# Hybrid encoder block on one core: who issues the stores of the FFN products, and when the residual is fetched

## Chip, cores and metric

The kernel runs on one core of a Trainium2 chip. The metric is the device time of one execution in microseconds. A core has a matrix engine (TensorE, here PE), three engines for element-wise work (VectorE or DVE, ScalarE or ACT, GpSimd or POOL) and SyncE (SP), which in this kernel only issues DMAs. Each engine works through its own instructions in order, and so does the queue of DMAs that an engine issues; an instruction whose wait isn't over holds all that stands behind it on its engine.

## What is computed

One encoder block on x of 1024 x 1024 floats: a SwiGLU FFN half, two token mixers with a merge, a second FFN half, a gated projection of per-layer embeddings p, and a final norm. D_FF is 2816.

```python
h = x
h = h + 0.5 * swiglu(rms_norm(h, ffn1_norm), ffn1_w_gate, ffn1_w_up, ffn1_w_down)
u = rms_norm(h, mix_norm)
...                                   # attention, retention, merge: h = h + merged @ w_out
h = h + 0.5 * swiglu(rms_norm(h, ffn2_norm), ffn2_w_gate, ffn2_w_up, ffn2_w_down)
gate = sigmoid(rms_norm(h, ple_norm) @ w_ple_gate)
h = h + gate * (p @ w_ple_proj)
return rms_norm(h, final_norm)

def swiglu(x, w_gate, w_up, w_down):
    return (silu(x @ w_gate) * (x @ w_up)) @ w_down
```

## The kernel before

**Matrix products.** Every float product is made of three matmuls: each operand is split into a high part h and a rest l, and h·h, h·l and l·h are added. Weights go through the class `Weights`. A load brings a piece of 128x1024 from memory into one of a few raw buffers (`wraw`); a fill splits it into a slot's `wh` (ACT, L144) and `wl` (DVE, L146; for some jobs POOL). Loads run as far ahead as raw buffers are free, fills as far as slots are free. `matrix` (L168 on) takes two raw pieces, top and bottom, and has POOL make two more from them, sums (L184, L185) and differences (L192, L193): seven factors in four fills.

**The FFN halves.** `Seven` computes each FFN as block products of two by two with seven products instead of eight. Its stage `products` runs over 11 pairs `j` of 256 of the 2816 columns: 14 products of 12 matmuls each (168), first for the gate, then for up. ACT moves the first part of a sum out of PSUM (`ev`, L576), DVE adds the others (L580), ACT applies silu (L602), DVE multiplies by up (L605). That gives four gated blocks `g` of 128x512. POOL makes three combinations of them (L627 to L630), and SP stores seven factors in memory, `hf` (L633). For the pair's part of the down matrix, `down_factors` loads four tiles `wd` (L645, SP), POOL makes four differences (L646 to L649), and SP stores them, `wf` (L651). The stage `down` then runs seven products (A11, A12, S2, S1, S3, S4, A22), each over the 11 `j` with 12 matmuls (132); it loads the stored factors again through `Weights.plain` (L155). The results are added to the residual `hres` (L672), which is x itself in FFN1 and a stored h in FFN2. The stages of FFN1 lie from about 68 to 532 us (products) and from there (down) in the profile, those of FFN2 from 1853 and from 2321 us.

**Head.** Ahead of the first products stage x is normed and turned, and p is projected: 16 blocks, which ACT takes from PSUM and SP stores in `ppspill` (L759, L760).

**Order.** PE runs in program order. On the other engines a scheduler sets the order from the program; on each DMA queue the issues stand in that order. So a load on SP stands behind whatever store was put ahead of it, and a store waits on SP until its data are made. Residual loads stand in the program ahead of `down`: 16 of 128x512 (L796 in FFN1, L1548 in FFN2).

Of the kernel before, what the change touches and what calls it, by code (L numbers as in the profile page):

```python
# [277 lines left out]
def hybrid_block_kernel(  # L278
# [29 lines left out]

    LEFT = ["A11", "A12", "S2", "S1", "S3", "S4", "A22"]
# [3 lines left out]
    def seven_jobs(name, wg, wu, wd):  # L313
# [9 lines left out]
        for a in LEFT:  # L323
            for j in range(NJ2):
                q = LEFT.index(a)
                t = {"S1": 0, "S2": 1, "S3": 2, "A22": 3}.get(a)
                if t is None:
                    f, c = {"A11": (0, 0), "A12": (1, 0), "S4": (1, 512)}[a]
                    wap = krows(wd, c, c + 512, 2 * j + f, 2 * j + f + 1)
                else:  # L330
                    wap = wsp[name][j][:, t:t + 1]
                W.plain((name, a, j), 1, D, False, [(0, 512, hsp[name][j][:, q:q + 1]), (512, D, wap)])
# [150 lines left out]
    class Seven:  # L483
# [66 lines left out]
        def products(self, between):  # L550
# [8 lines left out]
            g = {0: [ev.tile([P, 512], F32, name=f"g{i}") for i in range(4)]}  # L559
# [47 lines left out]
            for j in range(NJ2):  # L607
                h = g[j % 2]
# [9 lines left out]
                if j == 0:  # L618
                    self.top.close()
                    sp = self.top.enter_context(tc.tile_pool(name="hid2", bufs=1, side="right"))  # L620
                    g[1] = [sp.tile([P, 512], F32, name=f"g{i}") for i in range(4)]
                for _ in up or blocks("u", j, times(h)):
                    pass
                s1, s2, s4 = (sp.tile([P, 512], F32, name=f"s{i}", tag="s", bufs=8) for i in range(3))
# [6 lines left out]
                made = dict(A11=h11, A12=h21, S2=s2, S1=s1, S3=h12, S4=s4, A22=h22)  # L631
                for q, n in enumerate(LEFT):
                    nc.sync.dma_start(hsp[self.name][j][:, q], made[n])  # L633
                self.down_factors(sp, j)
# [4 lines left out]
        def down_factors(self, pool, j):  # L639

            gp = nc.gpsimd
            b11, b12, b21, b22 = t = [pool.tile([P, 512], F32, name=f"wd{i}", tag="s", bufs=8) for i in range(4)]
            for i in range(4):
                c0 = 512 * (i % 2)
                nc.sync.dma_start(t[i], krows(self.wd, c0, c0 + 512, 2 * j + i // 2, 2 * j + i // 2 + 1)[:, 0])  # L645
            gp.tensor_tensor(b11, b12, b11, op=OP.subtract)  # L646
            gp.tensor_tensor(b12, b22, b12, op=OP.subtract)  # L647
            gp.tensor_tensor(b22, b22, b11, op=OP.subtract)  # L648
            gp.tensor_tensor(b21, b21, b22, op=OP.subtract)  # L649
            for q, d in enumerate((b11, b22, b12, b21)):  # L650
                nc.sync.dma_start(wsp[self.name][j][:, q], d)  # L651

        def down(self, hres, finished, turn, other={}):
# [3 lines left out]
            def run(a, ps, start, stop, between=None):  # L657
                for j in range(NJ2):
                    key = self.name, a, j
                    h, l = (x[:, 0] for x in W[key])  # L660
                    for i in range(4):
# [12 lines left out]
            run("A11", sums, True, False)  # L674
            to(sums, 0, 0)
            pc = [bank("dn", "pdc") for _ in range(4)]
            run("A12", pc, True, True)
            to(pc, 0, 0)
            run("S2", sums, False, False)
            to(sums, 0, 1)  # L680
            pc = [bank("dn", "pdc") for _ in range(4)]
            run("S1", pc, True, False)
# [39 lines left out]
    order = [b + 4 * e for b in range(4) for e in range(2)]  # L722
    W.limit = 2
    W.load()
    load_p(0)
    seven.open()
    for b in order[:2]:
        load_x(b)
    seven.load_gain()
    W.load()  # L730
    load_p(2)
    for b in order[2:4]:
        load_x(b)
    nc.vector.memset(mhalf, -0.5)
# [19 lines left out]
    def proj_p(b, i):  # L754
# [5 lines left out]
        nc.sync.dma_start(ppspill[:, b, half(i)], t)  # L760
# [33 lines left out]
    for i in range(2):  # L794
        for b in range(NB):
            nc.sync.dma_start(hres[:, b, half(i)], x0[tok(b), half(i)])  # L796
# [59 lines left out]
    seven.down(hres, finished, turn, {4: lambda: W.drop(raws)})  # L856
# [689 lines left out]
    for i in range(2):  # L1546
        for b in range(NB):
            nc.sync.dma_start(hres[:, b, half(i)], h2spill[:, b, half(i)])  # L1548
# [13 lines left out]
    seven.down(hres, finished, turn)  # L1562
# [85 lines left out]
```

## Time and profile before

| | us |
|---|---|
| median of 3 runs (2648.21 to 2649.6) | 2648.36 |
| the profiled execution | 2651.99 |
| its span | 2650.2 |

| engine | busy us | share of span |
|---|---|---|
| PE | 2489.3 | 94% |
| DVE | 1514.1 | 57% |
| ACT | 1100.8 | 42% |
| POOL | 899.4 | 34% |

The mean granted clock of PE is 0.975 of full speed, 2.4 GHz. A busy share is a mean over stages with different limits: PE at 94% says that the engine is rarely idle, and the waits of PE say where it is. All DMAs of this kernel are issued by hardware queues (272,064 packets, 347.27 MB); POOL issues none. Times in the trace are from the start of the span.

### The profile page before, as it was taken

What the parts mean: (1) busy time and instruction counts of PE and PEld (TensorE: products, weight loads), DVE (VectorE), ACT (ScalarE), POOL (GpSimd) and SP (SyncE); (2) the same over time, 40 slices, a digit from 0 to 9 for tenths busy, and PEclk for the clock granted to TensorE, in tenths of its full rate; (3) what the DMA queues carried; (4) which work ended last, traced back from release to release, by engine and by line L of the source; (5) the groups of instructions that cost most, each with busy time, mean ns of one, the idle gap of its engine ahead of it and who ended that gap; (6) DMA issues with size and microseconds to landing.
All of it is one profiled execution on the core that took longest, in us unless ns stands there. A gap on an engine that the chain in (4) does not pass through costs nothing. (4 is left out here: it accounts for less than half of the span.)

```text
span 2650.2 us, 32857 instructions
## 1 busy us (share of the span) xinstructions
PE 2489.3 (94%) x11464; PEld 2030.7 (77%) x11464; DVE 1514.1 (57%) x2640; ACT 1100.8 (42%) x1900; POOL 899.4 (34%) x688
## 2 busy tenths in 40 slices
PE   6999999989999998989999999998999999989998
PEld 5777777768888777767878887787777777768887
DVE  5444444455567879997457664635444444445564
ACT  5333333334355667652235653414323233334452
POOL 5356565410000333343443431004456565410000
PEclk8999999989999999989999999999999999989999
DMA  5244344576640221221221218642244444586632
GB/s 194 92 135 158 130 146 139 172 261 212 192 155 21 84 81 33 68 80 44 86 82 37 82 61 244 183 161 82 94 133 147 130 156 138 174 296 203 196 98 95
DMA packets 272230, 349.36 MB, mean 132 GB/s; under 512 B 22976, under 2 KB 152256, under 8 KB 272064
## 3 DMA queue, kind: packets, MB, share of 16 engines
q1 hardware_dynamic: 272064, 347.27, 41.3%
q8 instruction: 90, 1.47, 0.2%
q14 instruction: 76, 0.62, 0.1%
HBM read 246.00 MB, written 101.19 MB: 131 GB/s over the span
## 5 line engine op out<-in xcount | busy, mean ns | idle before, releaser
L146 DVE TENSOR_TENSOR wl<-wraw,wh 128x1024 fp32r<-128x1024 f32 (+2 forms) x422 | 521.0, 1241 | 542.9 <-ACT wh L144 528.2
L144 ACT ACTIVATE wh<-wraw 128x1024 fp32r<-128x1024 f32 (+1 forms) x466 | 436.5, 938 | 852.1 <-PE pc L565 195.1
L439 PE MATMUL prod<-wh,uh 128*128 128x512 f32 (+1 forms) x648 | 266.6, 411 | 0.2 <-ACT gt L1036 0.2
L439 PE MATMUL prod<-wh,ul 128*128 128x512 f32 (+1 forms) x648 | 257.8, 398 | 0.0
L439 PE MATMUL prod<-wl,uh 128*128 128x512 f32 (+1 forms) x648 | 257.3, 397 | 0.0
L565 PE MATMUL pa<-th,wh 128*128 128x512 f32 x352 | 142.8, 406 | 43.2 <-ACT ev L576 43.2
L1029 PE MATMUL pgate<-uh,wh 128*128 128x512 f32 x384 | 159.2, 415 | 20.9 <-ACT gt L1036 19.8
L663 PE MATMUL pda<-wh 128*128 128x512 f32 x352 | 140.3, 399 | 21.4 <-ACT wh L144 10.7
L465 POOL TENSOR_TENSOR nst<-nst,mhalf 128x1 f32<-128x1 f32 x16 | 8.7, 550 | 443.6 <-DVE nst L464 443.6
L1029 PE MATMUL pgate<-uh,wl 128*128 128x512 f32 x384 | 154.5, 402 | 0.0
L1029 PE MATMUL pgate<-ul,wh 128*128 128x512 f32 x384 | 154.4, 402 | 0.0
L439 PEld LDWEIGHTS prod<-wh,ul 128*128 128x128 f32 x648 | 123.7, 191 | 29.2
L565 PE MATMUL pa<-ul,wh 128*128 128x512 f32 x352 | 141.2, 401 | 4.7 <-DVE ul L402 4.7
L1096 ACT ACTIVATE bias<-bias 128x1024 bf16<-128x1024 bf16 (+3 forms) x132 | 117.3, 890 | 63.0 <-DVE bias L1095 61.7
L146 POOL TENSOR_TENSOR wl<-wraw,wh 128x1024 fp32r<-128x1024 f32 x44 | 109.7, 2496 | 98.5 <-ACT wh L144 97.9
L565 PE MATMUL pa<-th,wl 128*128 128x512 f32 x352 | 142.7, 405 | 0.0
L565 PE MATMUL pa<-uh,wh 128*128 128x512 f32 x352 | 140.6, 399 | 1.8 <-ACT uh L401 1.8
L565 PE MATMUL pa<-tl,wh 128*128 128x512 f32 x352 | 142.0, 403 | 0.0
L663 PE MATMUL pda<-wl,wh 128*128 128x512 f32 x352 | 139.5, 396 | 2.5 <-DVE wl L146 2.5
L565 PE MATMUL pa<-uh,wl 128*128 128x512 f32 x352 | 140.8, 400 | 0.0
L565 PE MATMUL pc<-uh,wl 128*128 128x512 f32 x352 | 139.7, 397 | 0.0
L565 PE MATMUL pc<-ul,wh 128*128 128x512 f32 x352 | 139.6, 396 | 0.0
(274 smaller groups left out, 6008.0 us busy)
## 6 DMA issues: line engine op xcount, KB each, us to landing
wraw<-hf SPq DMA_DIRECT2D x154, 256.0 KB, 3.0
wraw<-in_ffn_w_gate_dram SPq DMA_DIRECT2D x44, 512.0 KB, 5.2
wraw<-in_ffn_w_up_dram SPq DMA_DIRECT2D x44, 512.0 KB, 3.8
hf<-g SPq DMA_DIRECT2D x88, 256.0 KB, 2.3
wd<-in_ffn_w_down_dram SPq DMA_DIRECT2D x88, 256.0 KB, 4.3
wf<-wd SPq DMA_DIRECT2D x88, 256.0 KB, 2.6
wraw<-wf SPq DMA_DIRECT2D x88, 256.0 KB, 3.2
hf<-s SPq DMA_DIRECT2D x66, 256.0 KB, 2.0
```

The costliest lines, as they stand in the source:

```text
L144: self.nc.scalar.activation(h, src, AF.Copy)
L146: eng.tensor_tensor(l, src, h.bitcast(F32), op=OP.subtract)
L439: nc.tensor.matmul(box[0][:, :cols], a, w, start=k == 0 and i == 0, stop=k == nk - 1 and i == 2)
L465: nc.gpsimd.tensor_tensor(st[:, 1:2], st[:, 0:1], mhalf, op=OP.pow)
L565: nc.tensor.matmul(ps, x_, y_, start=start and k == 0 and i == 0, stop=stop and k == 3 and i == 2, skip_group_check=True)
L663: nc.tensor.matmul(ps[i], x_, y_, start=start and j == 0 and n == 0, stop=stop and j == NJ2 - 1 and n == 2, skip_group_check=True)
L1029: nc.tensor.matmul(box[0], a, m, start=k == 0 and j == 0, stop=k == KT - 1 and j == 2)
L1096: nc.scalar.activation(m, m, AF.Copy, accum_out=cnt[:, j:j + 1])
```

## The change

It changes who issues the stores, in what pieces, and where some loads stand.

1. In `products` the four `g` blocks become one tile, the three combinations two tiles, and the stored order of the factors (`HID`) is made to fit: POOL stores them with three DMAs per pair (1 MB, 512 KB, 256 KB) where SP had seven of 256 KB.
2. The `wd` loads go into a function of their own, `down_rows`, called ahead of the up blocks; they are four of 256 KB in runs of 1 KB. The differences become eight operations of 128x256, and POOL stores them with two DMAs per pair instead of four on SP.
3. The 16 residual loads become four groups of four, each at `j` = 4 of one of the first four runs of `down`. A copy of one column (128x1) on POOL out of the weights in use, ahead of each load, holds it until then.
4. `ppspill` is stored by ACT instead of SP.
5. At the start the loads of p and x stand in another order.

```diff
+    HID = ["A11", "S3", "A12", "A22", "S2", "S1", "S4"]
...
-                q = LEFT.index(a)
-                t = {"S1": 0, "S2": 1, "S3": 2, "A22": 3}.get(a)
+                q = HID.index(a)
+                t = {"S1": 0, "S3": 1, "A22": 2, "S2": 3}.get(a)
...
-            g = {0: [ev.tile([P, 512], F32, name=f"g{i}") for i in range(4)]}
+            g = {0: ev.tile([P, 4, 512], F32, name="g0")}
...
-                    g[1] = [sp.tile([P, 512], F32, name=f"g{i}") for i in range(4)]
+                    g[1] = sp.tile([P, 4, 512], F32, name="g1")
+                wd = self.down_rows(sp, j)
-                s1, s2, s4 = (sp.tile([P, 512], F32, name=f"s{i}", tag="s", bufs=8) for i in range(3))
+                sa, sb = (sp.tile([P, 2, 512], F32, name=f"s{i}", tag="s", bufs=5) for i in range(2))
+                s2, s1, s4 = sa[:, 0], sa[:, 1], sb[:, 0]
-                made = dict(A11=h11, A12=h21, S2=s2, S1=s1, S3=h12, S4=s4, A22=h22)
-                for q, n in enumerate(LEFT):
-                    nc.sync.dma_start(hsp[self.name][j][:, q], made[n])
-                self.down_factors(sp, j)
+                to = hsp[self.name][j]
+                gp.dma_start(to[:, 0:4], g[j % 2])
+                gp.dma_start(to[:, 4:6], sa)
+                gp.dma_start(to[:, 6], s4)
+                self.down_factors(wd, j)
-        def down_factors(self, pool, j):
+        def down_rows(self, pool, j):
+            wd = [pool.tile([P, 2, 2, 256], F32, name=f"wd{i}", tag="s", bufs=5) for i in range(2)]
+            for q in range(2):
+                for f in range(2):
+                    rows = krows(self.wd, 0, D, 2 * j + f, 2 * j + f + 1)[:, 0].rearrange("p (i c) -> p i c", i=2)
+                    nc.sync.dma_start(wd[q][:, f], rows[:, :, 256 * q:256 * q + 256])
+            return wd
+        def down_factors(self, wd, j):
-            b11, b12, b21, b22 = t = [pool.tile([P, 512], F32, name=f"wd{i}", tag="s", bufs=8) for i in range(4)]
-            for i in range(4):
-                c0 = 512 * (i % 2)
-                nc.sync.dma_start(t[i], krows(self.wd, c0, c0 + 512, 2 * j + i // 2, 2 * j + i // 2 + 1)[:, 0])
-            gp.tensor_tensor(b11, b12, b11, op=OP.subtract)
-            gp.tensor_tensor(b12, b22, b12, op=OP.subtract)
-            gp.tensor_tensor(b22, b22, b11, op=OP.subtract)
-            gp.tensor_tensor(b21, b21, b22, op=OP.subtract)
-            for q, d in enumerate((b11, b22, b12, b21)):
-                nc.sync.dma_start(wsp[self.name][j][:, q], d)
-        def down(self, hres, finished, turn, other={}):
+            for q in range(2):
+                b11, b12, b21, b22 = (wd[q][:, i // 2, i % 2] for i in range(4))
+                gp.tensor_tensor(b11, b12, b11, op=OP.subtract)
+                gp.tensor_tensor(b12, b22, b12, op=OP.subtract)
+                gp.tensor_tensor(b22, b22, b11, op=OP.subtract)
+                gp.tensor_tensor(b21, b21, b22, op=OP.subtract)
+                gp.dma_start(wsp[self.name][j][:, :, 256 * q:256 * q + 256],
+                             wd[q].rearrange("p f i c -> p (f i) c"))
+        def down(self, hres, residual, finished, turn, other={}):
-            def run(a, ps, start, stop, between=None):
+            def fetch(t, i):
+                def go(h):
+                    for b in range(4 * t, 4 * t + 4):
+                        nc.gpsimd.tensor_copy(hres[:, b, 512 * i:512 * i + 1], h[:, 0:1].bitcast(F32))
+                        nc.sync.dma_start(hres[:, b, half(i)], residual(b, i))
+                return go
+            def run(a, ps, start, stop, between=None, load=None):
+                    if load and j == 4:
+                        load(h)
...
-            run("A11", sums, True, False)
+            run("A11", sums, True, False, load=fetch(0, 0))
-            run("A12", pc, True, True)
+            run("A12", pc, True, True, load=fetch(0, 1))
-            run("S2", sums, False, False)
+            run("S2", sums, False, False, load=fetch(1, 1))
-            run("S1", pc, True, False)
+            run("S1", pc, True, False, load=fetch(1, 0))
...
     order = [b + 4 * e for b in range(4) for e in range(2)]
+    seven.open()
+    load_p(0)
+    W.limit = 1
+    W.load()
+    load_x(order[0])
+    load_x(order[1])
+    seven.load_gain()
     W.limit = 2
     W.load()
-    load_p(0)
-    seven.open()
-    for b in order[:2]:
-        load_x(b)
-    seven.load_gain()
-    W.load()
-    load_p(2)
     for b in order[2:4]:
         load_x(b)
+    load_p(2)
     nc.vector.memset(mhalf, -0.5)
...
-        nc.sync.dma_start(ppspill[:, b, half(i)], t)
+        nc.scalar.dma_start(ppspill[:, b, half(i)], t)
...
-    for i in range(2):
-        for b in range(NB):
-            nc.sync.dma_start(hres[:, b, half(i)], x0[tok(b), half(i)])
...
-    seven.down(hres, finished, turn, {4: lambda: W.drop(raws)})
+    seven.down(hres, lambda b, i: x0[tok(b), half(i)], finished, turn, {4: lambda: W.drop(raws)})
...
-    for i in range(2):
-        for b in range(NB):
-            nc.sync.dma_start(hres[:, b, half(i)], h2spill[:, b, half(i)])
```

Three places show how this moves instructions: a pair of the products on SP and on POOL, the start of `down` on SP, and the head on DVE. A row is the line, the operation, what it writes and reads, and the shape of a tile; names carry a number, rows of a kernel its own lines. First SP in a middle pair of FFN1's products: `wd` are the tiles of the down matrix, `wf11` the stored factors of a pair, `wraw` the raw weight buffers. Before:

```order
L645 DMA wd0_1200<-in_ffn1_w_down_dram 128x512
L645 DMA wd1_1201<-in_ffn1_w_down_dram 128x512
L645 DMA wd2_1202<-in_ffn1_w_down_dram 128x512
L645 DMA wd3_1203<-in_ffn1_w_down_dram 128x512
L172 DMA wraw0_135<-in_ffn1_w_gate_dram 128x4x256
L651 DMA wf11_87<-wd0_1200 128x512
L651 DMA wf11_87<-wd1_1201 128x512
L651 DMA wf11_87<-wd3_1203 128x512
L651 DMA wf11_87<-wd2_1202 128x512
L172 DMA wraw1_136<-in_ffn1_w_gate_dram 128x4x256
L172 DMA wraw0_135<-in_ffn1_w_up_dram 128x4x256
```

After:

```order
L648 DMA wd0_1316<-in_ffn1_w_down_dram 128x2x256 x2
L172 DMA wraw0_135<-in_ffn1_w_gate_dram 128x4x256
L648 DMA wd1_1317<-in_ffn1_w_down_dram 128x2x256 x2
L172 DMA wraw1_136<-in_ffn1_w_gate_dram 128x4x256
L172 DMA wraw0_135<-in_ffn1_w_up_dram 128x4x256
L172 DMA wraw0_65<-in_ffn1_w_up_dram 128x4x256
```

The two gate loads had four `wd` loads ahead of the first and four factor stores between them; now there are two `wd` loads ahead of each, and no store.

On POOL in the same place, from the first combination of `g` on; L184, L185, L192 and L193 are the sums and differences of raw weights, `hf11` the stored gated factors, `s` the combinations. Before:

```order
L627 TENSOR_TENSOR s0_1186<-g1_840,g3_842 128x512
L628 TENSOR_TENSOR s1_1187<-s0_1186,g0_839 128x512
L629 TENSOR_TENSOR g1_840<-g0_839,g1_840 128x512
L184 TENSOR_TENSOR wraw1_136<-wraw0_135,wraw1_66 128x512
L185 TENSOR_TENSOR wraw1_136<-wraw1_136,wraw0_135 128x512
L630 TENSOR_TENSOR s2_1188<-g2_841,s1_1187 128x512
L193 TENSOR_TENSOR wraw0_65<-wraw1_66,wraw1_136 128x512
L646 TENSOR_TENSOR wd0_1200<-wd1_1201,wd0_1200 128x512
L647 TENSOR_TENSOR wd1_1201<-wd3_1203,wd1_1201 128x512
L648 TENSOR_TENSOR wd3_1203<-wd3_1203,wd0_1200 128x512
L649 TENSOR_TENSOR wd2_1202<-wd2_1202,wd3_1203 128x512
L192 TENSOR_TENSOR wraw1_66<-wraw0_135 128x512
```

After:

```order
L630 TENSOR_TENSOR s0_1181<-g1_836 128x512
L631 TENSOR_TENSOR s0_1181<-s0_1181,g1_836 128x512
L632 TENSOR_TENSOR g1_836<-g1_836 128x512
L184 TENSOR_TENSOR wraw1_136<-wraw0_135,wraw1_66 128x512
L636 DMA hf11_76<-s0_1181 128x1024
L185 TENSOR_TENSOR wraw1_136<-wraw1_136,wraw0_135 128x512
L633 TENSOR_TENSOR s1_1182<-g1_836,s0_1181 128x512
L193 TENSOR_TENSOR wraw0_65<-wraw1_66,wraw1_136 128x512
L635 DMA hf11_76<-g1_836 128x2048
L637 DMA hf11_76<-s1_1182 128x512
L656 TENSOR_TENSOR wd0_1316<-wd0_1316 128x256
L192 TENSOR_TENSOR wraw1_66<-wraw0_135 128x512
```

Three store issues now stand between POOL's operations, one ahead of the second sum L185 and two ahead of the `wd` work; the `wd` work that begins here is that of the next pair's `wd`, and its two stores follow behind these rows, ahead of the next L184.

SP where `down` of FFN1 begins; `hf` and `in_ffn1_w_down` are the loads of stored factors and of the down matrix, `cs` a table for later. Before:

```order
L651 DMA wf110_96<-wd3_3563 128x512
L651 DMA wf110_96<-wd2_3562 128x512
L155 DMA wraw0_135<-in_ffn1_w_down_dram 128x512
L155 DMA wraw0_65<-hf19_84 128x512
L155 DMA wraw0_65<-in_ffn1_w_down_dram 128x512
L796 DMA hres_3605<-in_x_dram 128x512 x16
L797 DMA cs_3597<-in_cst_dram 128x616
L155 DMA wraw1_66<-in_ffn1_w_down_dram 128x512
L155 DMA wraw1_136<-hf10_75 128x512
```

After:

```order
L815 DMA cs_3536<-in_cst_dram 128x616
L155 DMA wraw0_135<-hf18_83 128x512
L155 DMA wraw0_135<-in_ffn1_w_down_dram 128x512
L155 DMA wraw0_65<-hf19_84 128x512
L155 DMA wraw0_65<-in_ffn1_w_down_dram 128x512
L155 DMA wraw1_136<-in_ffn1_w_down_dram 128x512
L672 DMA hres_3544<-in_x_dram 128x512 x3
L155 DMA wraw0_135<-hf11_76 128x512
L155 DMA wraw0_135<-in_ffn1_w_down_dram 128x512
L155 DMA wraw0_65<-hf12_77 128x512
L155 DMA wraw0_65<-in_ffn1_w_down_dram 128x512
```

The 16 residual loads stood together behind two factor stores and ahead of the weight loads for later `j`; now three of the first four stand behind six or more of those loads, and no store is in the row.

DVE in the head, around the scaling of one x tile (`xt_491`, whose factor `nst_512` POOL makes): L402 before and L403 after is the split of turned blocks for PE. Before:

```order
L402 TENSOR_TENSOR tl_147<-ntr_426,th_146 128x4x128
L402 TENSOR_TENSOR tl_147<-ntr_443,th_146 128x4x128
L516 TENSOR_SCALAR nst_512<-nst_512 128x1
L518 SCALAR_TENSOR_TENSOR xt_491<-xt_491,nst_512,gain_155 128x1024
L402 TENSOR_TENSOR tl_147<-ntr_460,th_146 128x4x128
L402 TENSOR_TENSOR ul_121<-ntr_467,uh_120 128x4x128
L402 TENSOR_TENSOR ul_121<-ntr_484,uh_120 128x4x128
L402 TENSOR_TENSOR pt1_508<-ptr_502,pt0_507 128x512
```

After:

```order
L403 TENSOR_TENSOR tl_144<-ntr_426,th_143 128x4x128
L403 TENSOR_TENSOR tl_144<-ntr_443,th_143 128x4x128
L403 TENSOR_TENSOR tl_144<-ntr_460,th_143 128x4x128
L403 TENSOR_TENSOR ul_121<-ntr_467,uh_120 128x4x128
L403 TENSOR_TENSOR ul_121<-ntr_484,uh_120 128x4x128
L403 TENSOR_TENSOR pt1_508<-ptr_502,pt0_507 128x512
L517 TENSOR_SCALAR nst_512<-nst_512 128x1
L519 SCALAR_TENSOR_TENSOR xt_491<-xt_491,nst_512,gain_155 128x1024
```

The pair of `nst_512` and `xt_491` stood ahead of four splits and now stands behind them.

## Rows read from the trace of the kernel before

**Rows 1.** The page's first part: busy us (share of the span), instructions.

```profile
PE 2489.3 (94%) x11464; PEld 2030.7 (77%) x11464; DVE 1514.1 (57%) x2640; ACT 1100.8 (42%) x1900; POOL 899.4 (34%) x688
```

**Rows 2.** PE's waits, two windows: us in total, times, longest.

```profile
PE pa L565 <- ACT ev L576: 20.9, 9, 2.7
...
PE pa L565 <- ACT ev L576: 22.3, 9, 4.2
```

**Rows 3.** Stretches: length, engines' busy us (instructions), PEclk, DMA share, GB/s.

```profile
142.60:479.60 337.00, 318.20 (x1344) 255.26 (x1344) 152.98 (x161) 105.83 (x161) 193.62 (x129) 0.98 0.44 144
...
479.60:532.50 52.90, 52.89 (x229) 42.96 (x230) 24.87 (x29) 16.58 (x24) 20.09 (x15) 1.00 0.52 171
...
532.50:579.90 47.40, 34.47 (x133) 26.18 (x132) 18.42 (x26) 12.55 (x12) 12.75 (x8) 0.87 0.83 279
...
1930.40:2268.70 338.30, 319.29 (x1344) 256.07 (x1344) 151.29 (x161) 105.85 (x161) 193.84 (x129) 0.98 0.44 143
...
2321.60:2365.60 44.00, 32.96 (x133) 26.39 (x132) 13.06 (x13) 11.27 (x12) 10.89 (x8) 0.84 0.91 313
...
2365.60:2395.50 29.90, 29.90 (x133) 24.75 (x133) 20.65 (x20) 14.78 (x14) 0.00 (x0) 1.00 0.79 262
```

**Rows 4.** PE's timeline, one pair: start, us, instruction [idle before <-releaser].

```profile
310.31 0.50 PE L565 MATMUL pa<-th,wh 128*128 128x512 f32 x1 [2.74 <-ACT ev L576]
```

**Rows 5.** ACT's timeline, the same pair.

```profile
308.13 0.63 ACT L144 ACTIVATE wh<-wraw 128x512 fp32r<-128x512 f32 x1 [7.50 <-DMA wraw<-in_ffn_w_gate_dram]
```

**Rows 6.** Timeline of SP's queue, the same pair.

```profile
291.59 1.87 SPq L645 DMA_DIRECT2D wd<-in_ffn_w_down_dram  x4
...
293.56 0.38 SPq L172 DMA_DIRECT2D wraw<-in_ffn_w_gate_dram  x1
...
297.61 6.04 SPq L651 DMA_DIRECT2D wf<-wd  x4
...
303.74 0.39 SPq L172 DMA_DIRECT2D wraw<-in_ffn_w_gate_dram  x1
```

**Rows 7.** DVE's timeline, the same pair.

```profile
294.59 1.23 DVE L146 TENSOR_TENSOR wl<-wraw,wh 128x1024 fp32r<-128x1024 f32 x1 [4.55 <-ACT wh L144]
```

**Rows 8.** POOL: timeline of that pair; groups (busy, mean ns | idle, releaser).

```profile
281.25 2.21 POOL L627 TENSOR_TENSOR s<-g,g 128x512 f32<-128x512 f32 x1 [5.94 <-DVE g L605]
...
309.53 1.62 POOL L185 TENSOR_TENSOR wraw<-wraw,wraw 128x512 f32<-128x512 f32 x1
...
L629 POOL TENSOR_TENSOR g<-g,g 128x512 f32<-128x512 f32 x11 | 14.2, 1295 | 0.0
...
L146 POOL TENSOR_TENSOR wl<-wraw,wh 128x1024 fp32r<-128x1024 f32 x44 | 109.7, 2496 | 98.5 <-ACT wh L144 97.9
```

**Rows 9.** Timelines from products to down: PE, SP, ACT, POOL.

```profile
573.71 0.80 PE L663 MATMUL pda<-wh 128*128 128x512 f32 x1 [9.37 <-ACT wh L144]
...
555.49 10.41 SPq L796 DMA_DIRECT2D hres<-in_x_dram  x16
...
572.60 1.06 ACT L144 ACTIVATE wh<-wraw 128x1024 fp32r<-128x1024 f32 x1 [13.74 <-DMA wraw<-in_ffn_w_down_dram]
...
532.48 2.20 POOL L627 TENSOR_TENSOR s<-g,g 128x512 f32<-128x512 f32 x1 [19.89 <-DVE g L605]
...
2320.47 2.22 POOL L627 TENSOR_TENSOR s<-g,g 128x512 f32<-128x512 f32 x1 [17.61 <-DVE g L605]
```

**Rows 10.** DMA issues: KB each, median us from issue to landing.

```profile
hspill<-hres SPq DMA_DIRECT2D x8, 512.0 KB, 5.3
...
hf<-g SPq DMA_DIRECT2D x88, 256.0 KB, 2.3
```

**Rows 11.** Timelines of the head: PE, DVE.

```profile
53.01 1.12 PE L749 MATMUL ptr<-ident,praw 128*128 128x128 f32 x4 [5.73 <-DVE tl L402]
...
51.07 1.28 DVE L518 SCALAR_TENSOR_TENSOR xt<-xt,nst,gain 128x1024 f32<-128x1024 f32 x1 [3.91 <-POOL nst L517]
...
52.27 0.69 DVE L402 TENSOR_TENSOR tl<-ntr,th 128x512 fp32r<-128x512 f32 x1
```

More of the change, by code (lines that the diff above doesn't have):

```diff
@@ L607, in products @@
             for j in range(NJ2):
-                h = g[j % 2]
+                h = [g[j % 2][:, i] for i in range(4)]
                 gate, up = blocks("g", j, silu(h)), None
@@ L1561, in hybrid_block_kernel @@
     finished = normed(ple_norm[0], hres)
-    seven.down(hres, finished, turn)
+    seven.down(hres, lambda b, i: h2spill[:, b, half(i)], finished, turn)
     ph = ExitStack()
```

## Prediction

> **What bounds the kernel now.** I read the page's first part, PE's waits, tables by stage, and then one wait along its chain. The page's first part says that TensorE (PE) is busy 94% of the span [rows 1]: nothing shortens this kernel but filling PE's gaps, so an engine or a queue matters only where PE waits for it. The table of PE's waits, taken over each of the two products stages, shows one kind: PE at L565 waits for ScalarE's (ACT) eviction `ev`, nine times in each stage, 43.2 us together [rows 2], once per pair `j`. The tables by stretch price this. Eight pairs are 8 x 168 = 1344 matmuls and take 337.00 us in FFN1, 338.30 in FFN2; the stretch behind the first, without such a wait, 479.60 to 532.50, runs its 228 whole matmuls (229 shown, one cut by the edge) in 52.90 us, 0.232 each [rows 3]. At that rate 1344 take 311.8. So 25.2 and 26.5 us are lost, 51.7 over 16 pairs, **3.2 us for each**: about 2.3 of wait (43.2/18), the other 0.9 of work after it at a lower granted clock (0.98 against 1.00 over the stretch). Two further stretches are slow: the first run (A11) of each "down" stage, 132 matmuls, takes 47.40 and 44.00 us, at clock 0.87 and 0.84, where the run after it takes 29.90 at 1.00 [rows 3]. That is 17.5 and 14.1 lost.
>
> **Why PE waits in a pair.** Follow the one at 310.31 [rows 4]. ACT works in order. It is free from 300.6, but the next on it is the fill `wh<-wraw`, which waits 7.50 us for the pair's second gate load and starts at 308.13; the `ev` that PE needs stands behind that fill [rows 5]. SP issued that load at 303.74, though it issued the first at 293.56. Between them stand four stores of down factors, which hold SP from 297.61 to 303.65 [rows 6], because they wait for POOL's differences of `wd`, themselves waiting for loads issued only at 291.59. The raw buffer that the load fills was free at about 295.8, when DVE's `wl<-wraw` of 294.59 ended [rows 7].
>
> **Products, after.** The factor stores go to POOL and the `wd` loads go ahead of the up blocks, so SP has nothing between the two gate loads that waits for POOL's arithmetic; it keeps only two `wd` loads, whose buffers were stored from a pair earlier (some 40 us). The load goes out at about 296, when its buffer is free, and lands after its 4.4 us (303.74 to 308.13) at 300.4: as ACT comes to it at 300.6. ACT then gains 7.5 us and PE needs 2.3: the wait is gone, and the clock's share with it. ACT keeps 5 us of cover for what is late next, POOL (below). I take 3.0 of the 3.2, for 18 pairs: **54 us**.
>
> POOL is the price. It is busy 193.62 us in the eight pairs, 24.2 per pair [rows 3]. The eight half-wide `wd` operations I take as the four whole ones. Added are five DMA issues per pair. No row shows what POOL pays for one, X: the low end is what SP pays, 0.39 for a load [rows 6]; the high end is POOL's longest operation, 2.50 (L146, 128x1024); I take one POOL pass over a 512-wide tile, 1.30 (L629) [rows 8], since 128 to 512 descriptors are more than SP's one instruction and less than a pass over 1024. Then POOL has 24.2 + 6.5 = 30.7 per pair, under PE's 39.0 (168 x 0.232), and costs nothing on the average. Nearer is the order: all five issues stand ahead of the sums L184/L185 that feed a later fill of ACT. POOL starts the pair's chain at 281.25; its seven operations took to 292.4 (L627 2.21, the others 1.3 to 1.7), and with three issues (3.9) it is at 296.3; L192 (1.3), the `wd` work (6.0) and two issues (2.6) bring it to 306.2, the two sums to 309.1. Before, L185 ended at 311.15 and no PE wait came from it [rows 8]. So there are 2 us of room at least, and I guess twice that: X up to 1.7 to 2.2 is covered, beyond it ACT waits again. The same shape takes 2.21 us at L627 and 1.30 at L629 [rows 8]: something stretches POOL. Beside that stands the Trainium skill, "SBUF — State Buffer", section "SBUF: two separate sides": a DMA issued by GpSimd has its descriptors written by GpSimd, which some two-port DVE operations lock out; the same page gives 620 ns alone and 3100 ns beside such an operation. By 3.1 for every issue POOL would have 24.2 + 15.5 = 39.7 per pair, just over PE's 39.0; no run here shows it yet.
>
> SP loses eleven issues a pair (19 to 8); it doesn't bind, so that is worth nothing by itself. The larger stores and the 1 KB runs of `wd` move the same bytes; the DMA share is 0.44 in these stretches [rows 3], so nothing.
>
> **Down stages.** In FFN1 SP issues 16 residual loads from 555.49 to 565.90, behind two factor stores that wait for POOL; the first weight load comes after them, ACT's fill waits 13.74 us for it, and PE waits 9.37 at 573.71 [rows 9]. After, four residual loads stand at each of four later points, behind weight loads, and no store is on SP. What is late next: the fill of `j` = 4 goes into memory that held the last `g`, so it waits for the last `g` store, which POOL now issues behind its arithmetic. POOL starts L627 at 532.48 [rows 9]; three operations of 2.2, 2.2 and 1.3, another issue of 1.3 and L630's 1.3 bring the issue to about 541; 1 MB I estimate to land in 4 us, between 2.3 for 256 KB and 5.3 for 512 KB [rows 10]; then ACT's 1.06 and DVE's 1.23 [rows 9, 7]: 547.7. PE needs it at 532.5 + 48 x 0.232 = 543.6: a wait of 4.1, and some 1.5 of lower clock (at 0.9 for 2.3, as above). FFN1 gains 17.5 - 5.6 = 11.9. In FFN2 POOL starts its chain at 2320.47 [rows 9], 1.1 us ahead of the run, so 3.0 and 1.1 stay, and 10.0 are gained. Together **22 us**; bounds 2 (X of 2.5 and the 1 MB at four times 2.3 make either wait 7.6 longer) and 32 (all of it).
>
> **Head.** DVE's scaling at 51.07, which waits for POOL, stands ahead of the split at 52.27 for which PE waits 5.73 [rows 11]; DVE's new order puts four splits before it. Late `x` loads no longer stand behind spill stores on SP. Against that ACT issues the 16 spill stores, at 0.39 some 6 us of ACT work. I take **3**, bounds -4 (they fall on ACT where PE waits) and +6 (the wait).
>
> **Sum:** 54 + 22 + 3 = 79. The profiled execution lasted 2651.99 (span 2650.2): 2573. The median of the runs is 3.6 lower: 2569, so **2570**.
>
> **Rival B, another wait takes its place.** The pair's wait stays: X is 2.2 to 3.5, L185 comes late, ACT now waits for POOL's sums as it did for the load, and PE waits for `ev` as before. Only the other two gains are left: 2648.4 - 25 = **2624**; a half-way case lies near 2600. For it: POOL's longer operations, and cover of only 2 to 4 us. Against it: POOL is idle for 14.8 of a pair's 39.0 now. Here stands a rule of the Trainium skill, "DMA: Bandwidth & Descriptors", section "Issuing engines are not separate DMA queues": issuing from several engines saves only the time that the issue takes, usually small. By it the move to POOL would be worth little and 2624 the time. The trace speaks against it: the load was held 6.04 us by stores waiting in order [rows 6], and not by issue time.
>
> **Rival C, slower.** POOL becomes the engine that sets a pair's length, through its five issues. It does so for the worse once 24.2 + 5X is over today's 42.1 (337.00/8) plus 25/18 of what the rest gains: X over 3.9. At X of 5 a pair takes 49.2: 18 x 7.1 - 25 = +103, **2751**. For it: POOL's stretch beside DVE. Against: no row has a POOL operation longer than 2.5.
>
> **Rival D.** The last `g` store lands in time, the head gives its 6 and the products all 58: 2570 - 10 - 3 - 4 = **2553**.
>
> **How the numbers follow.** The forecast (2560 to 2598: X from 0.4 to 2.2, the transitions and the head between their bounds) has 0.56, B with its half-way case (2598 to 2632) 0.24, D 0.06; C 0.11; that losses I have not found cancel the gains, and the time stays, 0.03. The range leaves out the last two, and tails of the others: **2550 to 2632**. A measurement can tell 0.2% (5.3 us) from no change. Faster is forecast, B and D, 0.86; same 0.03; slower 0.11.
>
> **What would show it.** Right: no PE wait on `ev` in the products, eight pairs in about 313 us; the second gate load issued within 1 us of its buffer's release; POOL under 0.85 busy there; one PE wait of 2 to 5 us in each A11 run, on a fill that waits for the `g` store. Wrong: PE's waits on `ev` stay and ACT waits for L185 (B); POOL is busy throughout and pairs take over 42 us (C); no wait in A11 (D); a head longer than now.

## The result, and the profile after

The changed kernel takes 2581.51 us (median of 4 runs, 2578.19 to 2584.93) where the kernel before takes 2648.28: ratio 0.975, 95% interval 0.9733 to 0.9767. The prediction said 2570, within 2550 to 2632. The profiled execution lasted 2584.93 (span 2583.2).

The page's first part, and PE's waits over the whole span (us in total, times, longest). The 43.2 us of [rows 2] are gone; what is left at that line inside the pairs is 0.25 us at a time, 14 times, and there PE waits for DVE, not for ACT:

```profile
PE 2477.1 (96%) x11464; PEld 2022.7 (78%) x11464; DVE 1610.2 (62%) x2640; ACT 1102.7 (43%) x1900; POOL 1001.1 (39%) x918
```

```profile
PE pda L683 <- ACT wh L144: 5.5, 2, 3.0
...
PE pa L566 <- DVE ev L581: 3.4, 14, 0.3
```

The stretches that answer to [rows 3]: eight pairs of FFN1 and of FFN2, then the two A11 runs (columns as there; the two stretches of FFN2 take in three or four matmuls too many, some 0.9 us):

```profile
139.30:454.60 315.30, 313.57 (x1345) 252.06 (x1344) 192.02 (x160) 106.82 (x160) 224.10 (x201) 1.00 0.46 154
...
1893.80:2209.30 315.50, 314.06 (x1348) 252.72 (x1348) 190.42 (x161) 106.93 (x160) 224.08 (x201) 1.00 0.46 154
...
507.30:543.90 36.60, 33.12 (x133) 26.25 (x133) 24.19 (x40) 14.81 (x16) 12.06 (x15) 0.91 0.81 260
...
2262.00:2299.10 37.10, 34.15 (x137) 27.33 (x136) 17.05 (x16) 14.70 (x15) 12.95 (x15) 0.91 0.82 276
```

Both kernels issue the same matmuls in the same order, so the gain can be read off by the start of the same matmul in both traces:

| matmul | before | after | earlier by |
|---|---|---|---|
| second of the products, FFN1 | 69.71 | 69.47 | 0.2 |
| first of A11, FFN1 | 532.48 | 507.37 | 25.1 |
| first of A12, FFN1 | 579.93 | 544.11 | 35.8 |
| second of the products, FFN2 | 1857.47 | 1824.48 | 33.0 |
| first of A11, FFN2 | 2321.58 | 2262.24 | 59.3 |
| first of A12, FFN2 | 2365.64 | 2298.42 | 67.2 |

So the products give 24.9 + 26.3 = 51.2, the A11 runs 10.7 + 7.9 = 18.6, the head 0.2, and 2.8 are lost from A12 of FFN1 to the products of FFN2. Of the change only three of FFN1's four groups of residual loads lie there, and they cost nothing: the runs A12 to S4 take 29.9 us each. The same stretch differs from the kernel before by -3.2 to +3.2 in the profiled executions of the other kernels with the residual in four parts, so 2.8 is within the scatter of single executions.

One pair, on SP, DVE and ACT, answers to [rows 5 to 7]. The second gate load goes out at 285.17, as the split that frees its buffer ends (283.88 + 1.23), and ACT's fill at 291.06 waits for PE and no longer for a load:

```profile
279.28 0.37 SPq L172 DMA_DIRECT2D wraw<-in_ffn_w_gate_dram  x1
279.75 2.10 SPq L648 DMA_DIRECT2D wd<-in_ffn_w_down_dram  x2
285.17 0.37 SPq L172 DMA_DIRECT2D wraw<-in_ffn_w_gate_dram  x1
...
283.88 1.23 DVE L146 TENSOR_TENSOR wl<-wraw,wh 128x1024 fp32r<-128x1024 f32 x1 [1.18 <-ACT wh L144]
...
291.06 0.63 ACT L144 ACTIVATE wh<-wraw 128x512 fp32r<-128x512 f32 x1 [1.14 <-PE pa L566]
```

POOL's issues, which no row of before showed, and the start of `down` in FFN1 on POOL, ACT and PE; last, the page's issue row of the 1 MB store:

```profile
281.68 0.58 POOL L635 DMA_DIRECT2D hf<-g  x1
282.26 0.55 POOL L637 DMA_DIRECT2D hf<-s  x1
...
289.85 0.73 POOL L660 DMA_DIRECT2D wf<-wd  x1
...
515.04 0.58 POOL L635 DMA_DIRECT2D hf<-g  x1
...
520.46 2.00 ACT L144 ACTIVATE wh<-wraw 128x1024 fp32r<-128x1024 f32 x2 [5.49 <-DMA hf<-g]
...
521.57 0.80 PE L683 MATMUL pda<-wh 128*128 128x512 f32 x1 [3.02 <-ACT wh L144]
```

```profile
hf<-g POOLq DMA_DIRECT2D x22, 1024.0 KB, 5.6
```

An issue takes 0.55 to 0.73 us of POOL, and in FFN1 the fill of `j` = 4 waits for the last store of `g`, as the prediction had it. In FFN2 the trace puts this wait on the 256 KB store of `s` that POOL issues right behind the one of `g`.

### The profile page after: what moved, and what is told of

Read it like the earlier page. It is cut to its first block, busy times and chain, and to the rows that moved or that the text cites. A ratio compares the mean times of both kernels' runs of the same rounds, so it can differ in the third digit from the quotient of the medians.

```text
span 2583.2 us, 32690 instructions
## 1 busy us (share of the span) xinstructions
PE 2477.1 (96%) x11464; PEld 2022.7 (78%) x11464; DVE 1610.2 (62%) x2640; ACT 1102.7 (43%) x1900; POOL 1001.1 (39%) x918
## 4 chain that ended last, share of the span: by engine, by line
PE 75%; DVE 10%; issue 6%; ACT 4%; POOL 3%; DMA 2%; SPq 0%; ACTq 0%; POOLq 0%; DVEq 0%
PE pa L566 17%; PE pc L566 12%; PE prod L440 11%; PE pda L683 9%; PE pdc L683 7%; PE pgate L1047 7%; PE pmrg L396 4%; DVE wl L146 2%; DVE bias L1113 1%; ACT bias L1114 1%; PE ppt L1366 1%; PE plg L396 1%; PE ppv L1377 1%; PE psc L396 1%; ACT wh L144 1%
## 5 line engine op out<-in xcount | busy, mean ns | idle before, releaser
L146 DVE TENSOR_TENSOR wl<-wraw,wh 128x1024 fp32r<-128x1024 f32 (+2 forms) x422 | 619.2, 1469 | 425.6 <-ACT wh L144 421.3
L146 POOL TENSOR_TENSOR wl<-wraw,wh 128x1024 fp32r<-128x1024 f32 x44 | 109.7, 2496 | 98.4 <-ACT wh L144 97.9
L566 PE MATMUL pc<-uh,wh 128*128 128x512 f32 x352 | 139.2, 395 | 0.0
L440 PEld LDWEIGHTS prod<-wl,uh 128*128 128x128 f32 x648 | 124.5, 192 | 18.7
L440 PEld LDWEIGHTS prod<-wh,uh 128*128 128x128 f32 x648 | 124.4, 192 | 18.8 <-ACT gt L1054 0.3
L683 PE MATMUL pda<-wh,wl 128*128 128x512 f32 x352 | 139.0, 395 | 0.0
```

The costliest lines, as they stand in the source:

```text
L146: eng.tensor_tensor(l, src, h.bitcast(F32), op=OP.subtract)
L440: nc.tensor.matmul(box[0][:, :cols], a, w, start=k == 0 and i == 0, stop=k == nk - 1 and i == 2)
L566: nc.tensor.matmul(ps, x_, y_, start=start and k == 0 and i == 0, stop=stop and k == 3 and i == 2, skip_group_check=True)
L683: nc.tensor.matmul(ps[i], x_, y_, start=start and j == 0 and n == 0, stop=stop and j == NJ2 - 1 and n == 2, skip_group_check=True)
```

## Experiments

**Is it the stores' place in SP's queue?** First the four stores of down factors alone, out of the kernel before:

```diff
-                nc.sync.dma_start(wsp[self.name][j][:, q], d)
+                gp.dma_start(wsp[self.name][j][:, q], d)
```

> The kernel before with one edit: the four stores of down factors per pair (wf, 256 KB each) are issued by POOL, all else as it was (wd loads late, gated factors stored by SP in seven pieces, residual up front). Theory A (a load on SP stood behind stores that waited for POOL): the second gate load goes out when its buffer is free, PE's 18 waits on ev vanish, worth 51 us as in the changed kernel; in the A11 runs the 16 residual loads stay, so at most 5 us more: 2592 to 2600. Rival B (what counts is the wd loads' earlier place, or fewer and larger stores): the waits stay and the time is 2640 to 2650. Rival C (what counts is that SP is rid of eleven of 19 issues): a part in proportion, 4 of 11, 18 us: 2630.

Measured: 2590.9 us, ratio 0.9786 (0.9754 to 0.9818). Theory A holds; the time is 1 us under its range. Both gate loads now follow each other on SP, and eight pairs (1344 matmuls, one cut) run without a gap, 0.2315 us each; windows and SP's timeline:

```profile
139.50:450.60 311.10, 311.10 (x1345) 252.57 (x1344) 164.80 (x161) 107.57 (x160) 208.05 (x161) 1.00 0.46 156
```

```profile
281.22 2.70 SPq L172 DMA_DIRECT2D wraw<-in_ffn_w_gate_dram  x2
```

So four of a pair's 19 issues carry all that the products can give; size and number of the stores and the `wd` loads' place are not needed for it.

Then all eleven stores on POOL, in their old pieces; beside the edit above:

```diff
-                    nc.sync.dma_start(hsp[self.name][j][:, q], made[n])
+                    gp.dma_start(hsp[self.name][j][:, q], made[n])
```

> The kernel before with all eleven stores per pair (seven of gated factors, four of down factors, 256 KB each) issued by POOL; pieces, wd loads and residual as they were. Theory A: no more than the four stores of down factors give, 2590 to 2600; POOL pays 11 x 0.57 = 6.3 us per pair and has the room (24.2 + 6.3 of 39). Rival C (SP's number of issues): all of 51 us here and a third of it with four stores. Rival D (POOL's issues cost DVE or POOL more than their own 0.57 us): slower than with four stores by 5 us or more.

Measured: 2580.22 us, 0.9748 (0.9719 to 0.9777). The products take 311.10 again, so the other seven stores give them nothing, as A had it, and C falls. But the time is 10 us under A's range, which had no gain from the other stores anywhere. The difference to the run before lies in the down stages, read by first matmuls: A11 of FFN1 takes 39.7 us here and 32.4 there, A12 30.4 against 40.3, A11 of FFN2 42.1 against 46.8. With four stores on POOL the 16 residual loads still stand ahead of weight loads, and PE's wait only moves into A12. This is PE's wait there, in the run with four stores:

```profile
PE pdc L663 <- ACT wh L144: 5.8, 1, 5.8
```

So the two edited lines of this run give what the whole change gives (2580.22 and 2581.51 us). Against this run the changed kernel gains 8.8 us in the A11 runs and loses 9.3 in the products.

**Does it matter which engine issues?** The five stores of the changed kernel back on SP, and then in the same places `nc.scalar`, on ACT (the other two of `g` and `s` likewise):

```diff
-                gp.dma_start(to[:, 0:4], g[j % 2])
+                nc.sync.dma_start(to[:, 0:4], g[j % 2])
...
-                gp.dma_start(wsp[self.name][j][:, :, 256 * q:256 * q + 256],
+                nc.sync.dma_start(wsp[self.name][j][:, :, 256 * q:256 * q + 256],
```

> The changed kernel with its five stores per pair issued by SP again; their sizes, the buffers, the residual in four parts and the head stay as changed. The two stores of down factors then stand again between the two gate loads on SP. Theory A: the waits of PE on ev come back, 18 of about 2 us and the lower clock behind them: 2581 + 40 to 51, so 2620 to 2635. Rival B (larger pieces are what helped): 2575 to 2585. On the side: one split per pair on DVE, 128x512, takes 4.6 us in the changed kernel and 0.85 elsewhere; if descriptors that POOL writes hold it, it is short again here; if POOL's arithmetic beside it does, it stays long.

Measured: 2708.41 us, 1.0227 (1.0198 to 1.0255): A in kind, and far over its number. SP and ACT in one pair, and PE's waits:

```profile
316.38 4.68 SPq L660 DMA_DIRECT2D wf<-wd  x2
321.17 0.57 SPq L172 DMA_DIRECT2D wraw<-in_ffn_w_gate_dram  x1
...
325.93 0.63 ACT L144 ACTIVATE wh<-wraw 128x512 fp32r<-128x512 f32 x1 [9.74 <-DMA wraw<-in_ffn_w_gate_dram]
```

```profile
PE pa L566 <- ACT ev L577: 90.4, 18, 5.5
```

The two larger stores wait for all eight differences of `wd`, which now end later than the four did (23.7 us after POOL starts the pair's chain, against 22.1); the load stands behind them as before, ACT waits 9.74 instead of 7.50 us, and PE 5.0 instead of 2.4 each time.

> The changed kernel with its five stores per pair issued by ACT. Theory A (a store in a queue holds what stands behind it until its data are made; on POOL that costs nothing, since POOL makes them itself): on ACT the stores of gated factors stand ahead of the first ev of the next pair and wait for POOL's chain of some 9 us, so PE waits again, 3 to 8 us per pair: 2630 to 2720. Rival B (any queue other than SP will do): 2575 to 2590, and DVE's split is back at 0.85 us, since no descriptors are written by POOL.

Measured: 2674.84 us, 1.0085 (1.0065 to 1.0104): A. ACT holds the `ev` behind the stores of gated factors until POOL's chain has ended:

```profile
299.89 0.60 ACT L577 ACTIVATE ev<-pa 128x512 f32<-128x512 f32 x1 [7.73 <-POOL s L633]
```

```profile
PE pa L566 <- ACT ev L577: 64.4, 20, 3.2
PE pc L566 <- ACT ev L577: 11.0, 10, 3.1
```

**What else was in the change, alone,** each put into the kernel before. The residual in four parts, with the change's `fetch`, which the first four runs call, and both loops of 16 loads taken out:

```diff
+                    if load and j == 4:
+                        load(h)
...
-            run("A11", sums, True, False)
+            run("A11", sums, True, False, load=fetch(0, 0))
```

> The kernel before with the residual alone fetched in four parts, as changed; stores and wd loads stay on SP. Theory A (16 residual loads ahead of the weight loads are the larger part of what the first run of down loses): 5 to 10 us per FFN, 2628 to 2638. Rival B (the stores of down factors and the last store of gated factors, which wait for POOL, end as late, so the residual hides behind them): 0 to 3 us per FFN, 2642 to 2648. The waits of PE on ev in the products stay at 18 in either case.

Measured: 2637.84 us, 0.9952 (0.9937 to 0.9967). A for FFN1, B for FFN2: the A11 runs take 36.50 (from 47.40) and 44.60 (from 44.00). ACT in FFN2 waits as long as before; the releaser that the trace infers is an old transfer, so the cause is not read from it:

```profile
535.80:572.30 36.50, 33.02 (x133) 25.67 (x132) 18.26 (x26) 11.55 (x11) 13.64 (x12) 0.95 0.79 253
2310.20:2354.80 44.60, 32.98 (x133) 26.40 (x132) 16.95 (x15) 14.30 (x14) 16.23 (x16) 0.85 0.78 264
```

```profile
2331.35 2.95 ACT L144 ACTIVATE wh<-wraw 128x1024 fp32r<-128x1024 f32 x3 [10.41 <-DMA pp<-ppspill]
```

Then the head, with the change's new order of the first loads:

```diff
-        nc.sync.dma_start(ppspill[:, b, half(i)], t)
+        nc.scalar.dma_start(ppspill[:, b, half(i)], t)
```

> The kernel before with the changed head alone: p and x loads in the new order, ppspill stored by ACT. The prediction took 3 us. The profile of the changed kernel reaches the first matmul of the products 2.4 us earlier and gives 2.1 back one matmul later, where PE waits for a split on DVE. Theory A: nothing remains: 2646 to 2650. Rival B: 3 us: 2645. Only the trace tells these apart: PE's place at that matmul.

Measured: 2649.95 us, ratio 1.0 (0.9987 to 1.0013): nothing remains. PE reaches the products 2.1 us earlier and waits 2.1 longer at the second matmul. The kernel before, then this one:

```profile
69.71 0.79 PE L565 MATMUL pa<-ul,wh 128*128 128x512 f32 x1 [1.60 <-DVE ul L402]
...
65.47 0.49 PE L565 MATMUL pa<-uh,wh 128*128 128x512 f32 x1 [1.53 <-ACT uh L401]
69.67 0.80 PE L565 MATMUL pa<-ul,wh 128*128 128x512 f32 x1 [3.71 <-DVE ul L402]
```

DVE starts the two `wl` splits ahead of that one 1.0 us earlier, but they take 3.46 us where they took 2.48, so it ends as before; why they take longer was not tried.

**The wait that stayed in A11.** The last pair's combinations on DVE:

```diff
-                gp = nc.gpsimd
+                gp = nc.vector if j == NJ2 - 1 else nc.gpsimd
```

> The changed kernel with the four combinations of the last pair alone (j = 10, FFN1 and FFN2) made by DVE instead of POOL. Theory A: the fill of j = 4 in the first run of down waits for the last store of gated factors (5.5 us of wait on ACT, 2.5 to 3.0 on PE), which POOL's seven us of arithmetic hold up; on DVE four passes take 2.8 us, the stores land some 4 to 5 us earlier and PE's wait there vanishes: 3 to 5 us per FFN with the clock behind it, 2571 to 2576. Rival B (the next wait takes its place: the weight loads, for which ACT already waits 3.2 and 1.2 us in that run): no change, 2579 to 2584. Rival C: DVE's splits come late behind the four passes and PE waits for wl: slower by 2 to 6 us.

Measured: 2574.91 us, 0.9724 (0.9698 to 0.9751): A. The A11 runs take 32.50 and 34.20 us; FFN2 gains 2.0 of its 3 to 5 us, and 2.2 us of PE's waits stay there. Next the same with the eleven stores, the residual in four parts and the late `wd` loads of before:

> The kernel before with all eleven stores per pair on POOL in their old pieces (2580 measured for this alone), the residual in four parts, and the last pair's four combinations on DVE; head and wd loads as before. Theory A (the gains add: products as with the eleven stores, first runs of down as in the changed kernel with the last pair on DVE, 14.9 and 9.8 us instead of 7.8 and 2.0): 2580 - 15 = 2565, so 2562 to 2569. Rival B (the last pair's seven small stores on POOL, 0.55 us each, or late wd loads hold the same fill): 2572 to 2580.

Measured: 2586.86 us, 0.9753 (0.9736 to 0.977). A and B fall. The products take what they should; the A11 runs take 38.7 and 49.1 us where the last edit alone gave 32.5 and 34.2, and PE waits 3.6 and 15.9 us in them for ACT's fill. In FFN2's A11, POOL, ACT, PE:

```profile
2263.98 2.26 POOL L646 TENSOR_TENSOR wd<-wd,wd 128x512 f32<-128x512 f32 x1 [7.88 <-DMA wd<-in_ffn_w_down_dram]
...
2277.10 2.95 ACT L144 ACTIVATE wh<-wraw 128x1024 fp32r<-128x1024 f32 x3 [13.23 <-DMA wf<-wd]
...
2278.21 0.79 PE L673 MATMUL pda<-wh 128*128 128x512 f32 x1 [15.92 <-ACT wh L144]
```

The last pair's `wd` come late, so their factors are stored late, and the fill of `j` = 4, in whose memory they lie, waits for those stores. So the earlier `wd` loads seem to be good not for the products but for the start of `down` in FFN2. No run moved them alone, so their share is not shown; that the same holds FFN2 in the run with the residual alone is likely, not shown either.

**What an issue on POOL costs.** The stores of the changed kernel in 22 pieces:

```diff
-                gp.dma_start(to[:, 0:4], g[j % 2])
+                for n in range(4):
+                    for c in (0, 256):
+                        gp.dma_start(to[:, n, c:c + 256], g[j % 2][:, n, c:c + 256])
...
+                for n in range(4):
+                    gp.dma_start(wsp[self.name][j][:, n, 256 * q:256 * q + 256], wd[q][:, n // 2, n % 2])
```

> The changed kernel with its five stores per pair cut into 22 in the same order (14 of gated factors, eight of down factors, half or quarter as wide), all on POOL. It prices POOL's issue and the slow rival. One issue takes 0.55 to 0.73 us in the changed kernel: POOL goes from 28.0 to about 28.0 + 17 x 0.57 = 37.7 us per pair, just under PE's 39. Theory A (only POOL's own time counts, and the sums L184/L185 come late behind the issues): PE's waits return, 18 of 1 to 4 us: 2600 to 2650. Rival B (POOL's room hides it): 2580 to 2590. Rival C (each issue costs more than 0.6 us when they crowd, or holds DVE): POOL is the bound, over 2650.

Measured: 2573.61 us, 0.9711 (0.9696 to 0.9725): faster than the changed kernel, which no theory had. POOL is busy 284.30 of 315.30 us, 35 per pair, and PE waits for nothing (in the time of the changed kernel's 1344 matmuls it does 1361 whole ones):

```profile
139.30:454.60 315.30, 315.30 (x1362) 255.61 (x1361) 185.93 (x163) 108.81 (x162) 284.30 (x341) 1.00 0.48 155
```

So the changed kernel's products were 4 us per FFN above what they can be. The reason is in DVE. Of the changed kernel, DVE and POOL in one pair:

```profile
322.78 4.17 DVE L146 TENSOR_TENSOR wl<-wraw,wh 128x1024 fp32r<-128x1024 f32 x1 [1.15 <-ACT wh L144]
326.87 0.67 DVE L581 TENSOR_TENSOR ev<-ev,pa 128x512 f32<-128x512 f32 x1
...
321.20 0.55 POOL L637 DMA_DIRECT2D hf<-s  x1
321.76 0.75 POOL L656 TENSOR_TENSOR wd<-wd 128x256 f32<-128x256 f32 x1
...
325.94 1.60 POOL L659 TENSOR_TENSOR wd<-wd 128x256 f32<-128x256 f32 x1
327.50 0.74 POOL L657 TENSOR_TENSOR wd<-wd 128x256 f32<-128x256 f32 x1
328.19 0.72 POOL L660 DMA_DIRECT2D wf<-wd  x1
```

A split of 1.22 us lasts 4.17, while POOL works without a pause, and the sum behind it is what PE waits 0.25 us for. Two runs take half of the last diff each: only the stores of `wf` cut into eight, or only those of `g` and `s` into 14.

> The changed kernel with only the two stores of down factors per pair cut into eight of 128x256 (the three of gated factors stay). With 22 small stores the products ran without any wait of PE, 7 us faster than the changed kernel, where PE waits 0.25 us for DVE in 14 of 18 pairs: a split on DVE (L146, 1.22 us) lasts 4.2 us there, while POOL works through the differences of wd without a pause, behind the store of g. Theory A (that split is held by POOL's unbroken run behind a DMA issue; an issue between the operations lets DVE in): the long split and PE's 0.25 us vanish: 2572 to 2577. Rival B (what holds it is the large store of g with its many descriptors): no change, 2579 to 2584.

> The changed kernel with only the three stores of gated factors per pair cut into 14 of 128x256 (the two of down factors stay). Theory A (POOL's unbroken run of wd differences holds DVE's split): the run stays, so does the wait: 2579 to 2584. Rival B (the 1 MB store of g): the wait goes, 2572 to 2577.

Measured: 2573.07 us, 0.9701 (0.9682 to 0.9719), and 2574.05 us, 0.9712 (0.9693 to 0.9731). In both the products take 311.1 and 311.2 us and PE's 0.25 us are gone, so the second expectation by theory A missed. The same split on DVE with the stores of `wf` cut, and POOL's first issue beside it; then both with the other stores cut:

```profile
320.67 2.75 DVE L146 TENSOR_TENSOR wl<-wraw,wh 128x1024 fp32r<-128x1024 f32 x1 [1.15 <-ACT wh L144]
...
322.29 0.56 POOL L661 DMA_DIRECT2D wf<-wd  x1
```

```profile
321.31 1.23 DVE L146 TENSOR_TENSOR wl<-wraw,wh 128x1024 fp32r<-128x1024 f32 x1 [1.58 <-ACT wh L144]
...
320.74 2.14 POOL L640 DMA_DIRECT2D hf<-s  x4
```

Where POOL issues between its differences, the split ends 0.6 us after the first such issue (322.29 + 0.56). Where POOL issues small stores in a row, the split falls into that row and takes its 1.23. Both fit a split that is held while POOL computes and let in while it issues; neither run tells that apart from the store's size alone. The row of the changed kernel does not fit it: there the split ends at 326.95, 1.2 us ahead of POOL's next issue (328.19), and beside a difference that takes 1.60 us where those just ahead of it take 0.73 to 0.75. Shown is that smaller stores, of either kind, take PE's waits away; how DVE is let in stays open.

**Both together:** 22 pieces in the first ten pairs (the last pair keeps its three large stores of `g` and `s`), and the last pair's combinations on DVE.

```diff
+                if j < NJ2 - 1:
...
+                else:
+                    nc.gpsimd.dma_start(to[:, 0:4], g[j % 2])
```

> The changed kernel with both things that the runs so far point to: 22 small stores on POOL in the first ten pairs, and the last pair's four combinations on DVE with its three large stores. Theory A (the two gains are of different places and add): 2581.5 - 7.9 - 6.6 = 2567, so 2564 to 2570. Rival B (small stores leave the last pair's stores behind others on POOL, and the first run of down loses again what the products gain): 2572 to 2577.

Measured: 2568.56 us, 0.9689 (0.9674 to 0.9704): A, and the lowest median of these kernels (the interval overlaps that of the run with `wf` cut). Eight pairs and the two A11 runs:

```profile
139.10:450.50 311.40, 311.40 (x1345) 252.41 (x1344) 184.03 (x160) 107.64 (x160) 280.17 (x337) 1.00 0.49 156
503.30:535.40 32.10, 30.79 (x134) 24.59 (x133) 24.19 (x41) 14.36 (x16) 3.81 (x7) 1.00 0.84 279
2246.50:2281.00 34.50, 32.29 (x134) 25.88 (x133) 19.26 (x19) 14.36 (x14) 6.84 (x11) 0.95 0.84 292
```

## Why the prediction was right, and where its sum was off

The profiled execution gained 67.1 us where the sum had 79; by medians it is 66.8 against 78. Of the 12 us that are missing, the products, the A11 runs and the head have some 3 each; the last 3 lie within the scatter between the FFNs.

- **Products, 54: measured 51.2.** The mechanism was the one predicted, and four stores alone show it. The stall-free rate was right (311.8 forecast for eight pairs, 311.1 measured without waits). What the sum lacked was that POOL's issues change DVE: 3.4 us of new waits of PE for DVE and slower matmuls behind them, some 7 us together, gone in the runs with small stores. The prediction looked at POOL's time and did not ask who else slows down.
- **POOL's price, X = 1.30: measured 0.55 to 0.73,** near the low bound: 0.55 to 0.58 for a store of 128 rows, 0.73 for one of 512. POOL is at 28.0 us per pair (224.10/8), not 30.7, and rival C had no ground: 22 issues leave POOL at 35 and cost nothing. The rule of the Trainium skill's "SBUF — State Buffer" (section "SBUF: two separate sides"), by which GpSimd cannot write descriptors beside some DVE operations, is not seen in the issue times; the 3100 ns of that page of the Trainium skill, which the prediction set in for an issue, is the time of a whole DMA. The same section has the other direction too: of a GpSimd operation that reads SBUF and a DVE operation with two SBUF inputs, the one that starts first keeps the shared ports to its end and the other waits. The split has two such inputs (`wraw`, `wh`) and is held beside POOL, but for up to 4.6 us and over several of POOL's operations, not one.
- **A11 runs, 22: measured 18.6.** The wait was where the prediction put it and no longer than forecast (3.02 and 2.48 on PE, against 4.1 and 3.0). The store was issued 0.5 us sooner after POOL's start than forecast and took 5.4 us to ACT's fill, where 4 had been taken for its landing. (The forecast's terms add up to 547.3, not 547.7, so its wait should read 3.7.) The mis-sized term is the clock: 36.60 is 6.7 over 29.90; the waits (3.02, and 0.47 for `wl` right behind) explain 3.5, and 3.2 are matmuls at the lower clock, where 1.5 was taken by scaling from the pairs' mean (2.3 us of wait there; 43.2/18 is 2.4). From 0.6 us before that 3.02 us wait ends the granted clock is 0.50, its lower level of 1.2 GHz, for 6.8 us. In the eight pairs of FFN1 in the kernel before it was 0.50 behind three of the waits, for 3.4 us each time, and 1.00 behind the other five, so the pairs' mean was no measure for one wait. Also, the two FFNs were given one cause. The residual alone gives FFN1 its 11 us and FFN2 nothing.
- **Head, 3: measured 0.2.** PE did arrive 2.4 us earlier. The step that failed is that nothing was asked of what comes next: a split on DVE that ends when it ended before, since the splits ahead of it took 1.0 us longer.
- **Rival B and the rule on issuing engines.** By the Trainium skill, "DMA: Bandwidth & Descriptors", section "Issuing engines are not separate DMA queues", the move saves issue time only. The runs speak against it here: moving four issues of 0.4 us per pair is worth 57 us, and the same five stores give 2581.51, 2674.84 and 2708.41 us on POOL, ACT and SP. What differs is what stands behind the store while its data are made.

## What to carry to other kernels

Try a store in the queue of the engine that makes its data last: there it waits for nothing that the engine hadn't to do anyway, while on the other two queues tried here it held what stood behind it. Before you count on a wait removed, look one instruction further at the same engine (the head gave its 2 us back there), and count a wait of PE with the lower clock behind it, by a row of about its length and not by a mean. When work moves onto an engine that is idle half the time, look also at its neighbours' durations, not only at its own share.

## What the runs showed of the hardware that was not expected

DVE's split (L146) in the eight pairs of FFN1, duration min/median/max in ns, of the kernel before, the changed kernel, and the changed kernel with its stores on ACT:

```profile
L146 DVE TENSOR_TENSOR wl<-wraw,wh x81: 847/1219/2057, 141.1 to 478.1; 128x512 fp32r<-128x512 f32 x49, 128x1024 fp32r<-128x1024 f32 x32
```

```profile
L146 DVE TENSOR_TENSOR wl<-wraw,wh x80: 682/1224/4620, 140.2 to 452.5; 128x512 fp32r<-128x512 f32 x48, 128x1024 fp32r<-128x1024 f32 x32
```

```profile
L146 DVE TENSOR_TENSOR wl<-wraw,wh x80: 682/1182/1227, 146.7 to 497.1; 128x512 fp32r<-128x512 f32 x48, 128x1024 fp32r<-128x1024 f32 x32
```

With DMAs issued by POOL, a split of 128x512 can last 4.6 us; with the same POOL arithmetic and the stores on ACT none lasts over 1.23, on SP none over 1.76. So the hold comes with the issues on POOL; by what mechanism was not tried.

The same stores can also be compared by their landing, on POOL's queue and, with the changed kernel's stores back on SP, on SP's:

```profile
wf<-wd POOLq DMA_DIRECT2D x44, 512.0 KB, 3.6
```

```profile
wf<-wd SPq DMA_DIRECT2D x44, 512.0 KB, 3.5
hf<-g SPq DMA_DIRECT2D x22, 1024.0 KB, 3.9
```

The 512 KB of `wf` land as fast from either; the 1 MB of `g` takes 5.6 us from POOL's queue. From ACT's it takes 3.9 as well. So the 4 us that the prediction took for 1 MB is what the other two queues give.
